# Down layers of four MLPs: 24 of 32 k tiles as seven block products in place of eight

## The chip, the cores and the metric

The program runs on one core of a Trainium2 chip. The metric is the device time of one execution in microseconds (us), as the median of repeated runs. The engines are TensorE (PE in the profile, its weight loads PEld), VectorE (DVE), ScalarE (ACT), GpSimd (POOL) and SyncE (SP), which issues the DMAs. [...]

## The reference

Two model blocks of two layers each work on 512 tokens of 1024 channels, with short convolution, sparse attention, latent attention and differential attention. Each of the four layers ends in an MLP with a squared ReLU, and this is the part that the change touches:

```python
# first block, both layers
x = x + jnp.square(jax.nn.relu(hm @ w_up[layer])) @ w_down[layer]
# second block, both layers
x = _layernorm(DEEPNORM_ALPHA * x + _sqrelu_mlp(x, ffn_w_up[i], ffn_w_down[i]), ...)
```

w_up is 1024 x 4096 and w_down 4096 x 1024, all in f32.

## The kernel before

Tokens lie in four tiles of 128. The residual stream x is kept in SBUF as [128 tokens, 4 tiles, 1024]. Every f32 product is made of three matmuls in the fp32r type: an operand is split into a high part, a ScalarE copy into fp32r (line 95, tiles named ...h), and a low part, a VectorE subtraction (line 96, tiles named ...l). Then high x high, high x low and low x high are accumulated in a PSUM bank. All matmuls are issued by line 91. The split tiles come from one pool of six pairs of 128x1024, which up weights, down weights and r2 parts share; a pair is free when the last matmul that reads it is done. One pair is held by the memory keys of the second layer while the first MLP runs.

An MLP has two stages. The up stage (dense_b, line 221) makes 16 units of 256 hidden channels: a unit's weights are two blocks of 512 KB, its 48 matmuls of 128x512 fill the banks pus and put one after the other, ScalarE takes the ReLU (line 679), and VectorE multiplies it with the bank into r2 (line 680), which is kept for all 4096 channels in four tiles of 128x4096. While a unit runs, the weights of the next are loaded and split. The down stage (dense_a, line 165) then runs over 32 k tiles of 128 hidden channels: a row block of w_down of 512 KB is loaded and split, two k tiles of r2 are split at a time, and for each of the four token tiles six matmuls of 128x512 go to two banks; eight banks hold the whole result until the last k tiles. After that each token tile is added to x or goes into the LayerNorm with the factor ALPHA on x (lines 323 and 330).

The order within an engine is set by a scheduler that follows the order of the program text and takes an instruction when its inputs and buffers are there by its own costs. In each engine's queue instructions run strictly in that order. SP issues all loads; the raw weights have three buffers.

Of the kernel before, what the change touches and what calls it, by code (L numbers as in the profile page):

```python
# [10 lines left out]
FT = mybir.dt.float32  # L11
# [3 lines left out]
OP = mybir.AluOpType  # L15
# [17 lines left out]
def model_kernel(ctx: ExitStack, tc: tile.TileContext, I, out, tap=lambda *a: None, stop=0):  # L33
# [79 lines left out]
    def r16(name, dtype=FR):  # L113
        return big.tile([P, 4096], dtype, name=name, tag="r16")
# [50 lines left out]
    def dense_a(nK, lhs, weights, chunks, evac, tail=4, ntok=MT, late=None, ahead=3, hook=None):  # L165

        nch = len(chunks)
        dst = {}

        def alloc(t):  # L170
            if t in dst:
                return
            if nch == 2:
                if t == 0:
                    rot["S"] = rot["T"] = 0
                dst[t] = list(bankST("acc")) if t < 3 else [bankB("acc"), bankB("acc")]
            else:
                dst[t] = [bankT("acc") if t % 2 else bankS("acc")]

        W = {}  # L180

        def step(k, t, cs=range(nch)):
            alloc(t)
            wh, wl = W[k]
            lh, ll = lhs(k, t)
            for a, b, st, sp in ((lh, wh, k == 0, False), (lh, wl, False, False), (ll, wh, False, k == nK - 1)):
                for c in cs:
                    c0, c1 = chunks[c]
                    mm(dst[t][c][:, :c1 - c0], a, b[:, c0:c1], st, sp)

        head = max(0, nK - tail)
        k0 = 0
        if late is not None:
            k0 = min(ahead, nK)
            for k in range(k0):
                W[k] = weights(k)
            for t in range(ntok):
                if t == 2:
                    late()
                for k in range(k0):  # L200
                    step(k, t)
        for k in range(k0, head):
            W[k] = weights(k)
            for t in range(ntok):
                step(k, t)
        k0 = max(k0, head)
        for k in range(k0, nK):
            W[k] = weights(k)
        if hook:
            hook()  # L210
        for t in range(ntok):
            if nch == 2 and t == ntok - 1:
# [112 lines left out]
    def layer_norm(t, ps, gb, bb, alpha=ALPHA, dst=None):  # L325
        xt = x[:, t, :]
        st = small(4, "ln")
        for c in range(2):
            xc = x[:, t, c * 512:(c + 1) * 512]
            nc.vector.scalar_tensor_tensor(xc, xc, alpha, ps[c], op0=OP.mult, op1=OP.add, accum_out=st[:, c:c + 1])  # L330
        nmu = st[:, 2:3]
        nc.vector.scalar_tensor_tensor(nmu, st[:, 0:1], st[:, 1:2], ndiv, op0=OP.add, op1=OP.mult)
        sq = w4("sq")
        nc.scalar.activation(sq, xt, AF.Square, bias=nmu, accum_out=st[:, 3:4])
        xg = w4("xg")
        nc.vector.scalar_tensor_tensor(xg, xt, nmu, gb, op0=OP.add, op1=OP.mult)
        r = rstd_of(st[:, 3:4], 1, D, 1e-5)
        for c in (slice(0, 512), slice(512, D)) if dst is not None else (slice(0, D),):
            nc.vector.scalar_tensor_tensor(xt[:, c], xg[:, c], r, bb[:, c], op0=OP.mult, op1=OP.add)
            if dst is not None:  # L340
                nc.sync.dma_start(dst[:, c], xt[:, c])
# [325 lines left out]
                todo.append(unit)  # L667
        return todo

    def mlp(L, box, w_up, w_down, after, hook=None, tail=3):  # L670
        xT = box["xT"]
        r2 = [r16("r2", FT).rearrange("p (k n) -> p k n", k=8) for _ in range(4)]
        ups = dense_b(xT[0], xT[1], 8, 16,
                      lambda u, k0: wblk(w_up, 4096, k0, 4, u * 256, 256, base=L * D * 4096), box["late"], True)
        for u in range(16):
            ps = next(ups)
            rr = w4("rr").rearrange("p (a n) -> p a n", a=2)
            for m in range(2):
                nc.scalar.activation(rr[:, m, :], ps[m], AF.Relu)  # L679
                nc.vector.scalar_tensor_tensor(r2[u // 4][:, (2 * u) % 8 + m, :], ps[m], 0.0, rr[:, m, :],  # L680
                                               op0=OP.max, op1=OP.mult)
        rs = {}

        def lhs(k, t):
            if k not in rs:
                h, l = pair("r")
                h, l = (v.rearrange("p (a n) -> p a n", a=2) for v in (h, l))
                split(h, l, r2[k // 8][:, k % 8:k % 8 + 2, :])
                rs[k], rs[k + 1] = (h[:, 0], l[:, 0]), (h[:, 1], l[:, 1])
            return rs[k][0][:, t * P:(t + 1) * P], rs[k][1][:, t * P:(t + 1) * P]  # L690

        dense_a(32, lhs, lambda k: wcols(w_down, D, k, 0, D, base=L * 4096 * D), C2, after, tail=tail, hook=hook)


    rope_tab = {}
# [689 lines left out]
    after, box = ln_next(ln_rows("mix", 0), 1.0)  # L1385
    w_out(I["mla_w_o_2"], 0, oT, after, range(4, 8))
    tap("x4", x)
    after, box2 = ln_next(ln_rows("ffn", 0))
    mlp(0, box, I["ffn_w_up_2"], I["ffn_w_down_2"], after)
    xT = box2["xT"]  # L1390
    tap("x5", x)
    if stop == 3:
# [167 lines left out]
    rows_ = ln_rows("ffn", 1)  # L1560

    def after(t, ps):
        layer_norm(t, ps, *rows_, dst=out[0, t * P:(t + 1) * P, :])

    mlp(1, box, I["ffn_w_up_2"], I["ffn_w_down_2"], after, tail=4)


def bucket_onehots():
# [45 lines left out]
```

## Time and profile before

| what | value |
|---|---|
| median of 3 runs | 2416.0 us (2415.68 to 2416.78) |
| the profiled execution | 2416.09 us |
| its span, first to last instruction | 2414.3 us |
| mean granted TensorE clock | 0.995 of full speed |
| TensorE busy | 2358.9 us, 98% |
| VectorE busy | 1221.3 us, 51% |
| ScalarE busy | 969.4 us, 40% |
| GpSimd busy | 270.7 us, 11% |

A matmul's record overlaps the next one, since matmuls are pipelined; the pitch from start to start tells what one costs. In the rows below, a name such as wl<-raw,wh says what is written and what is read, a bracket at the end of a row of the timeline says how long the engine had been idle and what ended that, and GB/s is the last column of a row by stretch.

### The profile page before, as it was taken

The page shows a single profiled execution, that of the slowest core. Times are in us where ns is not written, and L with a number is a line of the kernel's source. Part 1 is how long each engine was busy: PE and PEld are TensorE (multiplying, and loading weights), DVE is VectorE, ACT ScalarE, POOL GpSimd, SP SyncE. Part 2 cuts the span into 40 slices and gives each one's busy share as a digit, 9 for nine tenths or more (in the row PEclk, how much of TensorE's full clock was granted, in tenths as well). Part 3 has the DMA queues.
Part 4 walks back from the last instruction along what each step waited for, and adds up shares of the span by engine and source line. Part 5 has one row for each costly group of instructions (what it writes and reads, how often), then busy time and mean ns, then how long its engine had stood idle before and what let it go on. Part 6 is the DMA issues. An engine that isn't in the chain of part 4 may idle for free.

```text
span 2414.3 us, 32343 instructions
## 1 busy us (share of the span) xinstructions
PE 2358.9 (98%) x12735; PEld 2030.2 (84%) x12735; DVE 1221.3 (51%) x2250; ACT 969.4 (40%) x1749; POOL 270.7 (11%) x458
## 2 busy tenths in 40 slices
PE   8999999999988999999999999999999999999998
PEld 7888888888887888888888888888889997888887
DVE  6564333336678973333347773333366668433334
ACT  5342322225458853332225543222235555323222
POOL 1110000000345520000001100000011222000000
PEclk9999999999999999999999999999999999999999
DMA  6233332334201133323221233323321222432332
GB/s 205 82 109 90 105 104 80 96 96 131 75 27 36 45 102 105 91 85 96 96 84 47 63 114 105 103 80 96 97 90 53 61 63 79 123 104 79 96 96 70
DMA packets 149540, 214.91 MB, mean 89 GB/s; under 512 B 12571, under 2 KB 119390, under 8 KB 149387
## 3 DMA queue, kind: packets, MB, share of 16 engines
q1 hardware_dynamic: 148718, 212.54, 28.5%
q8 instruction: 100, 1.64, 0.3%
q14 instruction: 54, 0.43, 0.1%
q10 hardware_dynamic: 668, 0.30, 0.0%
HBM read 210.68 MB, written 2.13 MB: 88 GB/s over the span
## 4 chain that ended last, share of the span: by engine, by line
PE 88%; DVE 5%; ACT 3%; POOL 2%; DMA 1%; issue 1%; ACTq 0%; DVEq 0%; POOLq 0%
PE pus L91 16%; PE put L91 16%; PE acc L91 13%; PE accs L91 12%; PE acct L91 12%; PE df L91 5%; PE sp L91 2%; PE wo L91 2%; PE pT L473 2%; PE do L91 1%; POOL z L457 1%; POOL rstd L129 1%; PE no L91 1%; PE qks L91 1%; PE lo L91 1%
## 5 line engine op out<-in xcount | busy, mean ns | idle before, releaser
L96 DVE TENSOR_TENSOR wl<-raw,wh 128x1024 fp32r<-128x1024 f32 (+3 forms) x363 | 436.9, 1205 | 528.3 <-ACT wh L95 525.7
L95 ACT ACTIVATE wh<-raw 128x1024 fp32r<-128x1024 f32 (+3 forms) x363 | 375.3, 1038 | 566.4 <-PE acc L91 317.5
L129 POOL TENSOR_TENSOR rstd<-var,mhalf 128x1 f32<-128x1 f32 (+3 forms) x91 | 77.7, 854 | 1712.2 <-DVE var L127 1712.2
L91 PE MATMUL pus<-xTh,wh 128*128 128x512 f32 (+1 forms) x664 | 241.5, 366 | 1.9 <-ACT xTh L95 1.0
L91 PE MATMUL pus<-xTh,wl 128*128 128x512 f32 (+1 forms) x664 | 240.9, 364 | 0.0
L91 PE MATMUL put<-xTh,wl 128*128 128x512 f32 (+1 forms) x664 | 240.7, 363 | 0.0
L91 PE MATMUL pus<-xTl,wh 128*128 128x512 f32 (+1 forms) x664 | 240.4, 364 | 0.3 <-DVE xTl L96 0.3
L91 PE MATMUL put<-xTl,wh 128*128 128x512 f32 (+1 forms) x664 | 240.3, 364 | 0.0
L91 PE MATMUL put<-xTh,wh 128*128 128x512 f32 (+1 forms) x664 | 239.9, 364 | 0.0
L96 DVE TENSOR_TENSOR rl<-r,rh 128x1024 fp32r<-128x1024 f32 x64 | 78.2, 1224 | 160.7 <-ACT rh L95 160.7
L91 PE MATMUL accs<-wh,rh 128*128 128x512 f32 x384 | 149.8, 390 | 0.9 <-ACT rh L95 0.9
L91 PE MATMUL acct<-wh,rh 128*128 128x512 f32 x384 | 149.8, 390 | 0.0
L91 PE MATMUL accs<-wl,rh 128*128 128x512 f32 x384 | 149.5, 389 | 0.0
L91 PE MATMUL accs<-wh,rl 128*128 128x512 f32 x384 | 149.3, 389 | 0.0
L91 PE MATMUL acct<-wl,rh 128*128 128x512 f32 x384 | 149.3, 389 | 0.0
L91 PE MATMUL acct<-wh,rl 128*128 128x512 f32 x384 | 149.1, 389 | 0.0
L680 DVE SCALAR_TENSOR_TENSOR r<-pus,rr 128x512 f32<-128x512 f32 x64 | 44.3, 691 | 203.7 <-ACT rr L679 203.7
L91 PEld LDWEIGHTS pus<-xTh,wh 128*128 128x128 f32 x664 | 125.2, 189 | 22.9 <-ACT xTh L95 2.3
L91 PEld LDWEIGHTS put<-xTh,wl 128*128 128x128 f32 x664 | 125.3, 189 | 19.7
L91 PEld LDWEIGHTS pus<-xTl,wh 128*128 128x128 f32 x664 | 125.1, 189 | 20.0 <-DVE xTl L96 0.5
L91 PEld LDWEIGHTS pus<-xTh,wl 128*128 128x128 f32 x664 | 125.3, 189 | 19.4
L91 PEld LDWEIGHTS put<-xTh,wh 128*128 128x128 f32 x664 | 125.0, 189 | 19.5
(451 smaller groups left out, 5119.3 us busy)
## 6 DMA issues: line engine op xcount, KB each, us to landing
raw<-in_w_up_dram SPq DMA_DIRECT2D x64, 512.0 KB, 3.8
raw<-in_w_down_dram SPq DMA_DIRECT2D x64, 512.0 KB, 3.4
raw<-in_ffn_w_up_dram SPq DMA_DIRECT2D x64, 512.0 KB, 4.5
raw<-in_ffn_w_down_dram SPq DMA_DIRECT2D x64, 512.0 KB, 3.5
raw<-in_diff_w_qkv_dram SPq DMA_DIRECT2D x24, 512.0 KB, 3.6
raw<-in_a_w_in_dram SPq DMA_DIRECT2D x20, 512.0 KB, 3.6
raw<-in_w_out_dram SPq DMA_DIRECT2D x16, 512.0 KB, 4.0
raw<-in_mem_w_kv_dram SPq DMA_DIRECT2D x8, 512.0 KB, 4.6
```

Of the source, the lines that this page charges most:

```text
L91: return nc.tensor.matmul(o, a, b, start=start, stop=stop, skip_group_check=True)
L95: nc.scalar.activation(h, src, AF.Copy)
L96: nc.vector.tensor_sub(l, src, h.bitcast(FT))
L129: nc.gpsimd.tensor_tensor(r, v, mhalf[:np_, :w], op=OP.pow)
L457: nc.gpsimd.tensor_scalar(z[:, b, :nq], z[:, b, :nq], rc[:, b:b + 1], sc[b], op0=OP.mult, op1=OP.mult)
L473: nc.tensor.transpose(T[:, c0:c0 + P], z[:, b, kt * P:(kt + 1) * P], ident)
L680: nc.vector.scalar_tensor_tensor(r2[u // 4][:, (2 * u) % 8 + m, :], ps[m], 0.0, rr[:, m, :], op0=OP.max, op1=OP.mult)
```

## The change

The first 24 of the 32 k tiles of a down layer are taken in three groups of eight. A group is a product of 512 tokens x 1024 channels with 1024 x 1024 weights, cut in two each way: blocks a11 to a22 of r2 (256 tokens x 512 channels) and b11 to b22 of w_down (512 x 512). In place of the eight block products there are seven, made of sums of blocks, with some results accumulated in the same banks: the Winograd form of Strassen's scheme. A group becomes ready with every fourth up unit, and its seven products are woven between the following four units, two behind each and one behind the last. A product has its operands (a load or block sums, then the splits sa and sb of one block of each side), 24 matmuls into two banks (sA or sB by turns), and an evacuation that adds the two banks to a quarter of x, which takes the factor ALPHA where a quarter is first met. A group is kept until the next one: r2 has two tiles in place of four, and the weights' four blocks are in two tiles rw, overwritten by sums. The last 8 k tiles are done by dense_a as before. In the second block the LayerNorm behind the MLP has the factor 1.0.

```diff
+    def seven(buf, k0, src, base, first, alpha):
+        a11, a12, a21, a22 = (buf[:, 4 * k:4 * k + 4, 256 * t:256 * t + 256] for t, k in ((0, 0), (0, 1), (1, 0), (1, 1)))
+        slots = [r16("rw", FT).rearrange("p (s k n) -> p s k n", s=4, k=2) for _ in range(2)]
+        b11, b12, b22, b21 = ([slots[q // 2][:, q % 2 * 2 + i] for i in range(2)] for q in range(4))
...
+        def load(b, kh, nh):
+            for i in range(2):
+                nc.sync.dma_start(b[i], dram(src, base + (k0 + 4 * kh + 2 * i) * P * D + nh * 512,
+                                             [[D, P], [P * D, 2], [1, 512]]))
+        def minus(dst, a, b):
+            for i in range(2):
+                nc.vector.tensor_sub(dst[i], a[i], b[i])
...
+        def product(key, b, a, op, fresh, rows, cols):
+            def operands():
+                if op:
+                    op()
+                o["a"] = parts(st[a] if isinstance(a, str) else a, 4, "sa")
+                o["b"] = [parts(v, 2, "sb") for v in b]
+            def products():
+                if fresh:
+                    bank[key] = [(bankF if key == "A" else bankB)("s" + key) for _ in range(2)]
+                ps = bank[key]
+                ah, al = o["a"]
+                for k in range(4):
+                    bh, bl = (v[:, k % 2, :] for v in o["b"][k // 2])
+                    for n, (p, q) in enumerate(((ah, bh), (ah, bl), (al, bh))):
+                        for t in range(2):
+                            mm(ps[t], p[:, k, t * P:(t + 1) * P], q, fresh and k == 0 and n == 0, k == 3 and n == 2)
+            def evacuation():
+                for t in range(2):
+                    xc = x[:, 2 * rows + t, cols * 512:cols * 512 + 512]
+                    if first and alpha is not None and (rows, cols) not in seen:
+                        nc.vector.scalar_tensor_tensor(xc, xc, alpha, bank[key][t], op0=OP.mult, op1=OP.add)
+                    else:
+                        nc.vector.tensor_add(xc, xc, bank[key][t])
...
+        def op5():
+            minus(b11, b12, b11)
+            st["s"] = quarter()
+            nc.vector.tensor_add(st["s"], a21, a22)
+            load(b21, 1, 0)
+        def op6():
+            minus(b11, b22, b11)
+            nc.vector.tensor_sub(st["s"], st["s"], a11)
+        def op3():
+            nc.vector.tensor_sub(st["s"], a12, st["s"])
+        def op7():
+            minus(b12, b22, b12)
+            st["s3"] = quarter()
+            nc.vector.tensor_sub(st["s3"], a11, a21)
...
+        return loads, [product("A", b11, a11, lambda: load(b22, 1, 1), True, 0, 0),
+                       product("B", b11, "s", op5, True, 1, 1),
+                       product("A", b11, "s", op6, False, 0, 1),
+                       product("B", b22, "s", op3, False, 0, 1),
+                       product("A", b12, "s3", op7, False, 1, 1),
+                       product("B", b21, a12, None, True, 0, 0),
+                       product("A", b21, a22, lambda: minus(b21, b21, b11), False, 1, 0)]
-    def mlp(L, box, w_up, w_down, after, hook=None, tail=3):
+    def mlp(L, box, w_up, w_down, after, hook=None, tail=3, alpha=None):
...
-        r2 = [r16("r2", FT).rearrange("p (k n) -> p k n", k=8) for _ in range(4)]
+        rot["on"] = False
         for u in range(16):
+            if u % 4 == 0:
+                if u:
+                    loads, todo = seven(r2, 2 * u - 8, w_down, wd, u == 4, alpha)
+                    loads()
+                r2 = r16("r2", FT).rearrange("p (k n) -> p k n", k=8)
             ps = next(ups)
...
+            for _ in range(2 if u % 4 < 3 else 1):
+                if todo:
+                    operands, products, evacuation = todo.pop(0)
+                    operands()
+                    for e in last:
+                        e()
+                    products()
+                    last[:] = [evacuation]
...
-        dense_a(32, lhs, lambda k: wcols(w_down, D, k, 0, D, base=L * 4096 * D), C2, after, tail=tail, hook=hook)
+        dense_a(8, lhs, lambda k: wcols(w_down, D, 24 + k, 0, D, base=wd), C2, after, tail=tail, hook=hook)
```

What the scheduler makes of it is seen in the queues. First, TensorE in the first MLP, where unit 4 ends and unit 5 begins; before, the units follow each other:

```order
L91 MATMUL put<-xTh,wh 128x512
L91 MATMUL put<-xTl,wh 128x512
L91 MATMUL put<-xTh,wl 128x512
L91 MATMUL pus<-xTh,wh 128x512
L91 MATMUL pus<-xTl,wh 128x512
```

Now, from the middle of product 1 of the first group (sA) to the first use of a low weight half (sbl) in product 2 (sB):

```order
L91 MATMUL sA<-sbl,sah 128x512 x2
L91 MATMUL sA<-sbh,sal 128x512 x2
L91 MATMUL sA<-sbh,sah 128x512 x2
...
L91 MATMUL pus<-xTh,wh 128x512
L91 MATMUL pus<-xTl,wh 128x512
L91 MATMUL pus<-xTh,wl 128x512
L91 MATMUL pus<-xTh,wh 128x512
L91 MATMUL sB<-sbh,sah 128x512 x2
L91 MATMUL pus<-xTl,wh 128x512
...
L91 MATMUL sB<-sbl,sah 128x512 x2
```

Ten matmuls of product 1, four of unit 5, two of product 2 and four more of unit 5 stand there; the rest of product 2, unit 5 and product 3 follow.

Second, VectorE at the same place of the first MLP; before, the splits of the up weights (wl) and the writes of r2 (r):

```order
L680 SCALAR_TENSOR_TENSOR r_1991<-pus,rr 128x512
L96 TENSOR_TENSOR wl<-raw,wh 128x1024 x2
L680 SCALAR_TENSOR_TENSOR r_1991<-put,rr 128x512
L680 SCALAR_TENSOR_TENSOR r_1991<-pus,rr 128x512
L96 TENSOR_TENSOR wl<-raw,wh 128x1024 x2
```

Now, from the split of product 1's second weight pair to that of product 3's first (L688 are sums of weight blocks, L739 and L742 of r2 blocks, L723 evacuations):

```order
L96 TENSOR_TENSOR sbl<-rw,sbh 128x1024
L688 TENSOR_TENSOR rw<-rw 128x1024
L96 TENSOR_TENSOR sal<-sq,sah 128x1024
L688 TENSOR_TENSOR rw<-rw 128x1024
L96 TENSOR_TENSOR sbl<-rw,sbh 128x1024 x2
L723 TENSOR_TENSOR x<-x,sA 128x512 x2
L688 TENSOR_TENSOR rw<-rw 128x1024
L96 TENSOR_TENSOR wl<-raw,wh 128x1024
...
L739 TENSOR_TENSOR sq<-sq,r_1990 128x1024
...
L742 TENSOR_TENSOR sq<-r_1990,sq 128x1024
L96 TENSOR_TENSOR sbl<-rw,sbh 128x1024 x2
```

Left out are a sum of weight blocks and a split of up weights, and between L739 and L742 two evacuations of sB with an r2 write between them and a split of a block sum.

Third, VectorE in the third MLP, around units 4 and 5. Before:

```order
L680 SCALAR_TENSOR_TENSOR r_12861<-put,rr 128x512
L680 SCALAR_TENSOR_TENSOR r_12862<-pus,rr 128x512
L96 TENSOR_TENSOR wl<-raw,wh 128x1024 x2
L680 SCALAR_TENSOR_TENSOR r_12862<-put,rr 128x512
L680 SCALAR_TENSOR_TENSOR r_12862<-pus,rr 128x512
```

Now, from the write of unit 4's first half to the split that product 2 uses first:

```order
L780 SCALAR_TENSOR_TENSOR r_13498<-pus,rr 128x512
L96 TENSOR_TENSOR sbl<-rw,sbh 128x1024
L688 TENSOR_TENSOR rw<-rw 128x1024 x2
L780 SCALAR_TENSOR_TENSOR r_13498<-put,rr 128x512
L96 TENSOR_TENSOR sal<-sq,sah 128x1024
L688 TENSOR_TENSOR rw<-rw 128x1024
L96 TENSOR_TENSOR sbl<-rw,sbh 128x1024
```

Here the split of product 1's second weight pair stands first, and TensorE's queue has products 1 and 2 of a group back to back, 24 matmuls each, with a whole up unit of 48 behind every two products.

## Rows read from the trace of the kernel before

**Rows 1.** page, engines: busy us (share of the span), instructions
```profile
span 2414.3 us, 32343 instructions
...
PE 2358.9 (98%) x12735; PEld 2030.2 (84%) x12735; DVE 1221.3 (51%) x2250; ACT 969.4 (40%) x1749; POOL 270.7 (11%) x458
```

**Rows 2.** page, chain that ended last: shares by engine, by line
```profile
PE 88%; DVE 5%; ACT 3%; POOL 2%; DMA 1%; issue 1%; ACTq 0%; DVEq 0%; POOLq 0%
...
PE pus L91 16%; PE put L91 16%; PE acc L91 13%; PE accs L91 12%; PE acct L91 12%; PE df L91 5%; PE sp L91 2%; PE wo L91 2%; PE pT L473 2%; PE do L91 1%; POOL z L457 1%; POOL rstd L129 1%; PE no L91 1%; PE qks L91 1%; PE lo L91 1%
```

**Rows 3.** busy time in MLP stretches: PE, PEld, DVE, ACT, POOL; clock, DMA
```profile
290.00:360.00 70.00, 70.00 (x311) 57.95 (x310) 25.51 (x27) 20.79 (x27) 0.00 (x0) 1.00 0.32 98
...
440.00:550.00 110.00, 110.00 (x487) 91.09 (x486) 37.01 (x31) 30.75 (x31) 0.00 (x0) 1.00 0.30 96
...
2260.00:2360.00 100.00, 100.00 (x443) 82.84 (x442) 33.33 (x28) 27.65 (x27) 0.00 (x0) 1.00 0.30 95
```

**Rows 4.** timeline, first down layer: start, length, instruction, wait before it
```profile
402.72 0.68 DVE L680 SCALAR_TENSOR_TENSOR r<-put,rr 128x512 f32<-128x512 f32 x1
...
403.45 0.19 PEld L91 LDWEIGHTS acct<-wh,rh 128*128 128x128 f32 x1 [0.26 <-DVE r L680]
...
405.66 0.63 PE L91 MATMUL acc<-wh,rl 128*128 128x512 f32 x2
...
406.12 0.39 PE L91 MATMUL accs<-wh,rh 128*128 128x512 f32 x1
...
406.32 1.06 ACT L95 ACTIVATE wh<-raw 128x1024 fp32r<-128x1024 f32 x1 [4.29 <-PE acc L91]
...
407.42 1.23 DVE L96 TENSOR_TENSOR wl<-raw,wh 128x1024 fp32r<-128x1024 f32 x1 [4.01 <-ACT wh L95]
...
409.98 0.39 PE L91 MATMUL acct<-wh,rl 128*128 128x512 f32 x1
```

**Rows 5.** groups by line and shape: count, busy us, mean ns, idle before
```profile
L96 DVE TENSOR_TENSOR wl<-raw,wh 128x1024 fp32r<-128x1024 f32 x341 | 418.3, 1228 | 515.7 <-ACT wh L95 513.4 <-issue 0.6 <-PE wo L91 0.6
...
L95 ACT ACTIVATE wh<-raw 128x1024 fp32r<-128x1024 f32 x341 | 359.2, 1057 | 549.2 <-PE acc L91 305.1 <-PE put L91 205.6 <-issue 10.9
...
L680 DVE SCALAR_TENSOR_TENSOR r<-pus,rr 128x512 f32<-128x512 f32 x64 | 44.3, 691 | 203.7 <-ACT rr L679 203.7
...
L339 DVE SCALAR_TENSOR_TENSOR x<-xg,rstd,gb 128x1024 f32<-128x1024 f32 x12 | 15.4, 1284 | 5.9 <-POOL rstd L129 5.8
...
L323 DVE TENSOR_TENSOR x<-x,accs 128x512 f32<-128x512 f32 x12 | 8.2, 684 | 13.5 <-PE accs L91 13.5
...
L746 DVE TENSOR_TENSOR qr<-rope 128x256 f32<-128x256 f32 x8 | 3.3, 417 | 0.1
...
L679 ACT ACTIVATE rr<-pus 128x512 f32<-128x512 f32 x64 | 38.3, 598 | 249.1 <-PE pus L91 249.1
```

**Rows 6.** DMA issues: count, KB each, us to landing
```profile
raw<-in_w_down_dram SPq DMA_DIRECT2D x64, 512.0 KB, 3.4
...
raw<-in_w_out_dram SPq DMA_DIRECT2D x16, 512.0 KB, 4.0
```

**Rows 7.** busy time by stretch around a pause of TensorE; clock
```profile
134.00:136.00 2.00, 0.97 (x9) 0.72 (x7) 0.94 (x2) 1.56 (x7) 0.00 (x0) 1.00 0.00 0
136.00:138.00 2.00, 0.99 (x4) 0.74 (x4) 1.29 (x3) 2.00 (x5) 1.25 (x3) 0.92 0.01 4
138.00:140.00 2.00, 2.00 (x9) 1.81 (x9) 1.85 (x3) 1.57 (x3) 0.60 (x2) 0.50 0.05 8
140.00:142.00 2.00, 2.00 (x8) 1.62 (x8) 1.34 (x2) 1.80 (x4) 0.00 (x0) 0.72 0.47 147
```

**Rows 8.** timeline of TensorE in that stretch
```profile
136.91 0.87 PE L91 MATMUL mo<-mpth,mkvl 128*128 128x256 f32 x2 [1.94 <-ACT mpth L95]
...
138.43 0.63 PE L91 MATMUL put<-xTh,wh 128*128 128x512 f32 x1
...
138.85 0.63 PE L91 MATMUL put<-xTl,wh 128*128 128x512 f32 x1
```

More of the change, by code (lines that the diff above doesn't have):

```diff
@@ L668, in w_out_part, with parts, quarter, loads @@
         return todo
-    def mlp(L, box, w_up, w_down, after, hook=None, tail=3):
+    def seven(buf, k0, src, base, first, alpha):
+        a11, a12, a21, a22 = (buf[:, 4 * k:4 * k + 4, 256 * t:256 * t + 256] for t, k in ((0, 0), (0, 1), (1, 0), (1, 1)))
+        slots = [r16("rw", FT).rearrange("p (s k n) -> p s k n", s=4, k=2) for _ in range(2)]
+        b11, b12, b22, b21 = ([slots[q // 2][:, q % 2 * 2 + i] for i in range(2)] for q in range(4))
+        bank = {}
+        seen = set()
+        st = {}
+        def load(b, kh, nh):
[5 more added lines that the diff above has]
+                nc.vector.tensor_sub(dst[i], a[i], b[i])
+        def parts(v, k, name):
+            h, l = pair(name)
+            h, l = (c.rearrange("p (k n) -> p k n", k=k) for c in (h, l))
+            split(h, l, v)
+            return h, l
+        def product(key, b, a, op, fresh, rows, cols):
+            o = {}
+            def operands():
[20 more added lines that the diff above has]
+                        nc.vector.tensor_add(xc, xc, bank[key][t])
+                seen.add((rows, cols))
+            return operands, products, evacuation
+        def quarter(name="sq"):
+            return w4(name).rearrange("p (k n) -> p k n", k=4)
+        def op5():
[12 more added lines that the diff above has]
+            nc.vector.tensor_sub(st["s3"], a11, a21)
+        def loads():
+            load(b11, 0, 0)
+            load(b12, 0, 1)
+        return loads, [product("A", b11, a11, lambda: load(b22, 1, 1), True, 0, 0),
[5 more added lines that the diff above has]
+                       product("A", b21, a22, lambda: minus(b21, b21, b11), False, 1, 0)]
@@ L671, in mlp @@
+    def mlp(L, box, w_up, w_down, after, hook=None, tail=3, alpha=None):
         xT = box["xT"]
-        r2 = [r16("r2", FT).rearrange("p (k n) -> p k n", k=8) for _ in range(4)]
+        wd = L * 4096 * D
         ups = dense_b(xT[0], xT[1], 8, 16,
                       lambda u, k0: wblk(w_up, 4096, k0, 4, u * 256, 256, base=L * D * 4096), box["late"], True)
+        rot["on"] = False
+        todo = []
+        last = []
+        r2 = None
         for u in range(16):
+            if u % 4 == 0:
[3 more added lines that the diff above has]
+                r2 = r16("r2", FT).rearrange("p (k n) -> p k n", k=8)
@@ L679, in mlp @@
                 nc.scalar.activation(rr[:, m, :], ps[m], AF.Relu)
-                nc.vector.scalar_tensor_tensor(r2[u // 4][:, (2 * u) % 8 + m, :], ps[m], 0.0, rr[:, m, :],
+                nc.vector.scalar_tensor_tensor(r2[:, (2 * u) % 8 + m, :], ps[m], 0.0, rr[:, m, :],
                                                op0=OP.max, op1=OP.mult)
+            for _ in range(2 if u % 4 < 3 else 1):
[6 more added lines that the diff above has]
+                    last[:] = [evacuation]
+        for e in last:
+            e()
+        rot["on"] = True
         rs = {}
@@ L687, in lhs @@
                 h, l = (v.rearrange("p (a n) -> p a n", a=2) for v in (h, l))
-                split(h, l, r2[k // 8][:, k % 8:k % 8 + 2, :])
+                split(h, l, r2[:, k:k + 2, :])
                 rs[k], rs[k + 1] = (h[:, 0], l[:, 0]), (h[:, 1], l[:, 1])
             return rs[k][0][:, t * P:(t + 1) * P], rs[k][1][:, t * P:(t + 1) * P]
-        dense_a(32, lhs, lambda k: wcols(w_down, D, k, 0, D, base=L * 4096 * D), C2, after, tail=tail, hook=hook)
+        dense_a(8, lhs, lambda k: wcols(w_down, D, 24 + k, 0, D, base=wd), C2, after, tail=tail, hook=hook)
     rope_tab = {}
@@ L1387, in model_kernel @@
     tap("x4", x)
-    after, box2 = ln_next(ln_rows("ffn", 0))
-    mlp(0, box, I["ffn_w_up_2"], I["ffn_w_down_2"], after)
+    after, box2 = ln_next(ln_rows("ffn", 0), 1.0)
+    mlp(0, box, I["ffn_w_up_2"], I["ffn_w_down_2"], after, alpha=ALPHA)
     xT = box2["xT"]
@@ L1562, in after @@
     def after(t, ps):
-        layer_norm(t, ps, *rows_, dst=out[0, t * P:(t + 1) * P, :])
-    mlp(1, box, I["ffn_w_up_2"], I["ffn_w_down_2"], after, tail=4)
+        layer_norm(t, ps, *rows_, alpha=1.0, dst=out[0, t * P:(t + 1) * P, :])
+    mlp(1, box, I["ffn_w_up_2"], I["ffn_w_down_2"], after, tail=4, alpha=ALPHA)
 def bucket_onehots():
```

## The prediction

> **What bounds the kernel now.** I read the engine totals first. TensorE is busy for 2358.9 of 2414.3 us, VectorE for half of the span, ScalarE for 40% [rows 1]. Since a busy TensorE need not be one that sets the time, I then read the chain that ended last: 88% of it is TensorE, and the named parts of it are the up products (pus, put) and the down products (acc, accs, acct), together 69% of the span [rows 2]. Third, the busy time by stretch, for a piece of an up layer and two of down layers: in all of them TensorE is busy 100% of the stretch at full clock, VectorE only 33 to 36%, GpSimd not at all, and the DMA engines run at 0.30 to 0.32 [rows 3]. So in these stages nothing but the number of matmuls counts, and the other engines have room. The pitch of the matmuls comes from the timeline: from 406.12 to 409.98 us stand 17 steps of 128x512, so 3.86 / 17 = 0.227 us each; a matmul's own 0.39 us overlaps the next one [rows 4].
>
> **What goes.** One group of eight k tiles took 8 x 4 x 2 x 3 = 192 matmuls. Seven products of 4 x 3 x 2 = 24 make 168. That is 24 fewer in each of three groups of each of four MLPs, 288 in all, of the same shape, on a path where TensorE never waits: 288 x 0.227 = 65.4 us.
>
> The Trainium skill, "TensorE: Matmul & The Clock Gate", section "Wait — 56ns, not 53.3ns?", gives 215.7 ns from start to start for 512 columns at full clock. By it the 288 would be worth 62.1 us; the trace has 0.227 us, 5% more, and I go by the trace.
>
> **What is added.** Per group, 21 splits (7 of block sums of r2, 14 of weight halves) stand where 12 stood (8 weights, 4 of r2): 9 more, each a ScalarE copy of 1.057 us and a VectorE subtraction of 1.228 [rows 5]. New are 12 sums of 128x1024 on VectorE and 14 reads of a PSUM bank into x (0.684 us, as line 323 does it [rows 5]). A sum with a plain f32 result of that size is not in the trace. From below it is bounded by the split, 1.228; from above by four times the small one of line 746, 4 x 0.417 = 1.67; the nearest at the full size and with an f32 result is line 339 with 1.284 [rows 5]. I take 1.23.
>
> The budget of one group, woven with four up units, is then: TensorE (192 + 168) x 0.227 = 81.8 us. VectorE (21 + 8) x 1.228 = 35.6, sums 14.7, evacuations 9.6, the up units' eight r2 writes 5.5: together 65.4 us, 80%. ScalarE 29 x 1.057 + 8 x 0.6 = 35.5 us. VectorE has room on the average and little at any one place; as it works in order, what counts is how long its queue is ahead of each split that a product waits for.
>
> **Where TensorE waits, first MLP.** The memory keys of the next layer hold one of the six split buffer pairs here, so the scheduler put pieces of the next up unit between the products. Between the first use of the low half of product 1's second weight pair and that of product 2 stand 10 + 4 + 2 + 4 = 20 matmuls, 4.54 us; on VectorE between the same two splits a sum, a split, a sum and the split that is wanted, 4 x 1.228 = 4.91. TensorE waits 0.37 us. From there to product 3's first split stand 61 matmuls (22 of product 2, 13 pus, 24 put, 2), 13.85 us, against nine operations of 1.228, four evacuations and an r2 write, 14.48 us: 0.63 us. Product 1 itself waits for a copy, an activation, an r2 write and a split behind the up unit's end, about 0.2. Products 4 and 6 wait for the evacuations in front of their split: a bank's last matmul ends 0.06 us before the next stream starts, then 0.03 + 2 x 0.684 + 1.228 + 0.05 makes 2.6 us against 11 matmuls, 2.5: 0.1 each. The hand-overs in these sums are those of the timeline: 0.03 us from a matmul's end to ScalarE, 0.04 on to VectorE, 0.05 back to TensorE [rows 4]. Together 1.4 us, three times: 4.2.
>
> **The other three MLPs.** With all six pairs products 1 and 2 stand back to back. The split of product 1's second pair ends 0.4 us before product 1 starts (its copy needs the weight pair that the put half returns at its eleventh of 24 matmuls: 13 x 0.227 before the end). Behind it stand two sums, an r2 write, a split, a sum and product 2's split, 5 x 1.228 + 0.69 = 6.83, so it is ready 6.4 + 0.05 us after the start of product 1; TensorE is there after 26 matmuls, 5.9 us. Wait 0.56 us, nine times: 5.0. Between the later products stand 48 up matmuls, 10.9 us, and I count no wait.
>
> **Loads.** They stay 512 KB each and are as many as before; in rows of 2 KB, as w_out's, which land in 4.0 us against 3.4 for w_down [rows 6]. The next group's loads wait on SP for the last sum of the old one, with up loads queued behind them; both are wanted a unit (10.9 us) later, and are costed at nothing. GpSimd has no queue here. LayerNorm only changes a factor.
>
> **Sum.** -65.4 + 4.2 + 5.0 = -56.2 us on the profiled execution's 2416.1 us (span 2414.3 and 1.8 around it), which is the median, 2416.0. Forecast 2360 us. If nothing waited: 2350.7.
>
> **Rivals.** (a) VectorE is later than counted. With sums of 1.67 the six sums on the counted ways of the first MLP add 2.7 us per group and the three of the others 1.3: 8 + 12 = 20 us. With a hand-over as long as the wait of 0.26 us at the start of a down layer [rows 4] at each of 84 products, 21 us. Either gives 2380, both 2401. For it speaks that 80% leaves little; against it that such rows keep their length in every stretch.
>
> (b) The slower side: VectorE's queue is one operation late at every product. It works in order, and an evacuation that has to wait for TensorE's last matmul holds the split behind it, which the next product wants. Then 84 x 1.228 = 103 us come on top: 2463. It decides from a mean wait of (65.4 - 9.2) / 84 = 0.67 us more per product. Against it: most evacuations stand behind the splits of the next product.
>
> (c) The loads of a group (four of 512 KB) land one behind the other, 4 x 4.0 = 16 us instead of within the 10.9 us of an up unit: 5.1 us in 12 groups, 61 us, 2421: no change. Against it: DMA engines at 0.3 busy [rows 3].
>
> (d) The new waits cost the clock. After a pause of 1.94 us at 135 us the granted clock went to 0.50, that is 1.2 GHz, and 0.72 in the 2 us behind [rows 7], and matmuls of 128x512 stood 0.42 us apart [rows 8]; some 1.7 us are lost at such a place. Once per group this is 21 us, 2381; at each of 84 products 143 us, 2503. Against it: in that stretch TensorE worked for 49% of 4 us, whereas here the longest wait counted is 0.63 us between long runs. The same page of the Trainium skill, "Part 1: The HAM clock gate", says that the clock is halved when the array has been idle and comes back with sustained work; the trace agrees, with 0.50 after the pause and 1.00 before.
>
> **How the numbers follow.** Chances: forecast 0.75 (own range 2350 to 2376), (a) 0.14, (b) 0.05, (c) 0.03, (d) 0.03. The range goes from 2349 (no wait, and the 0.26 us at the start of the down layers gone too) to 2388, which takes in half of (a). A change of 0.2% is what a measurement of this kernel can tell: 4.8 us. Faster takes in the forecast, (a) and part of (d): 0.90; the same 0.04, from (c) and the edge of (a); slower 0.06, from (b) and the rest of (d).
>
> **What would show it.** Right: 288 fewer matmuls, pitch 0.227 us in the woven stage, no idle time of TensorE over 1 us there, its waits naming the sbl splits and 5 to 20 us in all; VectorE 1221 + 108 x 1.228 + 144 x 1.23 + 168 x 0.684 = some 1645 us, ScalarE 969 + 114 = 1083. Wrong: sums far from 1.23 us, waits for rw loads, clock below 1.00 in the woven stretches, or idle time at most products.

## The result, and the profile after

The changed kernel takes 2353.0 us (median of 4 runs, 2352.0 to 2356.7) beside 2416.4 us for the kernel before on the same chip (4 runs): ratio 0.974, 95% interval 0.972 to 0.976. That is 63.4 us, where 56.2 were forecast; 2360 was predicted with a range of 2349 to 2388. In a later comparison the same kernel, unedited, came to 2353.5 us.

Of the page of the changed kernel, its span, the engine totals and the chain that ended last, by engine:

```profile
span 2350.3 us, 32274 instructions
PE 2293.5 (98%) x12447; PEld 1971.0 (84%) x12447; DVE 1608.7 (68%) x2670; ACT 1078.4 (46%) x1857; POOL 269.9 (11%) x458
PE 88%; DVE 4%; ACT 3%; POOL 2%; DMA 1%; issue 1%; ACTq 0%; SPq 0%; POOLq 0%; DVEq 0%
```

Against [rows 1] TensorE is busy for 65.4 us less and its matmuls are 288 fewer; the span is 64.0 us shorter. TensorE's 88% of the chain is what it was [rows 2]: the same engine sets the time, with less to do. The gain lies where the edit is: from its first up matmul to its last down matmul the first MLP takes 341.4 us before (236.54 to 577.98) and 326.7 after (235.15 to 561.84), 14.8 less, and the other three take 15.8, 15.7 and 15.7 less. That is 61.9 us; the rest of the 63.4 lies outside the MLPs. A matmul comes with a weight load, so 288 of each are gone, and the runs do not tell the two apart. The woven stages of the four MLPs, by busy time (PE, PEld, DVE, ACT, POOL; then clock, DMA share, GB/s):

```profile
280.00:515.20 235.20, 235.20 (x1032) 191.82 (x1031) 178.79 (x183) 99.20 (x108) 0.00 (x0) 1.00 0.26 83
927.70:1162.10 234.40, 234.40 (x1034) 193.44 (x1033) 178.70 (x190) 98.77 (x108) 0.00 (x0) 1.00 0.26 84
1453.00:1688.00 235.00, 235.00 (x1036) 193.99 (x1035) 176.93 (x183) 99.21 (x108) 0.00 (x0) 1.00 0.26 85
2063.00:2297.50 234.50, 234.50 (x1034) 193.54 (x1033) 176.57 (x182) 98.97 (x107) 0.00 (x0) 1.00 0.26 85
```

In [rows 3] VectorE was at 33 to 36% in such stretches; here it is at 76%, and TensorE is as full as before, at full clock. PE busy hides small waits: these rows are at 100%, though there are some. They show on the weight loads. From the list of waits, what the loads for bank B waited for (us in all, times, the longest):

```profile
PEld sB L91 <- DVE sbl L96: 3.8, 17, 0.3
PEld sB L91 <- ACT sbh L95: 1.9, 9, 0.2
```

And from the view of the tile sA, the only thing that those for bank A waited for (us, times):

```profile
  DVE sbl L96: 0.9, 3
```

These are 29 waits of 0.15 us and more at 84 products, none over 0.33 us, 6.6 us together; 20 of them lie in the first MLP. What TensorE loses by them is less: from the first product's first matmul to the first of the last eight k tiles the stages take 235.55, 234.43, 234.37 and 234.43 us. The same 1032 matmuls take 233.92 us where nothing waits (the last three MLPs of the kernel without sums, below). So the waits cost 1.6 us in the first MLP and 0.5 in each of the others, 3.1 in all.

Nine of the waits, all in the first MLP at products 2, 4 and 6, are for ScalarE's copy of the high half (sbh), which the prediction did not count. At product 4 of the first group that copy starts when a matmul of product 3 returns the buffer pair, and the weight load waits for it:

```profile
306.98 2.01 ACT L95 ACTIVATE sbh<-rw 128x1024 fp32r<-128x1024 f32 x2 [1.21 <-PE sA L91]
...
308.09 0.30 PEld L91 LDWEIGHTS sB<-sbh,sah 128*128 128x128 f32 x2 [0.21 <-ACT sbh L95]
```

The new operations, by line and shape (count, busy us, mean ns, idle before them):

```profile
L96 DVE TENSOR_TENSOR sbl<-rw,sbh 128x1024 fp32r<-128x1024 f32 x168 | 203.1, 1220 | 93.2 <-ACT sbh L95 90.9 <-DMA rw<-in_ffn_w_down_dram 2.3
L688 DVE TENSOR_TENSOR rw<-rw 128x1024 f32<-128x1024 f32 x96 | 116.0, 1218 | 0.8
L723 DVE TENSOR_TENSOR x<-x,sA 128x512 f32<-128x512 f32 x84 | 54.3, 681 | 3.7 <-PE sA L91 2.8
```

The loads that have a new shape (count, KB each, us to landing):

```profile
rw<-in_w_down_dram SPq DMA_DIRECT2D x48, 512.0 KB, 6.7
rw<-in_ffn_w_down_dram SPq DMA_DIRECT2D x48, 512.0 KB, 8.0
```

Sums (1.218 us) and evacuations (0.681; these read a PSUM bank, one of TensorE's accumulation banks, and add it to x) are what the prediction took. The loads are not: medians of 6.7 and 8.0 us to landing, where w_out's landed in 4.0 [rows 6]. Only one wait for them shows in the 168 splits, 2.3 us on VectorE.

### The profile page after: what moved, and what is told of

Its sections match the earlier page's. It is cut to its first block, busy times and chain, and to the rows that moved or that the text cites. A ratio compares the mean times of both kernels' runs of the same rounds, so it can differ in the third digit from the quotient of the medians.

```text
span 2350.3 us, 32274 instructions
## 1 busy us (share of the span) xinstructions
PE 2293.5 (98%) x12447; PEld 1971.0 (84%) x12447; DVE 1608.7 (68%) x2670; ACT 1078.4 (46%) x1857; POOL 269.9 (11%) x458
## 4 chain that ended last, share of the span: by engine, by line
PE 88%; DVE 4%; ACT 3%; POOL 2%; DMA 1%; issue 1%; ACTq 0%; SPq 0%; POOLq 0%; DVEq 0%
PE pus L91 17%; PE put L91 17%; PE sA L91 11%; PE sB L91 8%; PE acc L91 8%; PE df L91 5%; PE accs L91 4%; PE acct L91 4%; PE sp L91 2%; PE wo L91 2%; PE pT L473 2%; POOL z L457 1%; PE do L91 1%; POOL rstd L129 1%; PE no L91 1%
## 5 line engine op out<-in xcount | busy, mean ns | idle before, releaser
L96 DVE TENSOR_TENSOR wl<-raw,wh 128x1024 fp32r<-128x1024 f32 (+3 forms) x267 | 318.1, 1196 | 176.6 <-ACT wh L95 173.8
L95 ACT ACTIVATE wh<-raw 128x1024 fp32r<-128x1024 f32 (+3 forms) x267 | 273.6, 1031 | 265.6 <-PE acc L91 86.9
L96 DVE TENSOR_TENSOR sbl<-rw,sbh 128x1024 fp32r<-128x1024 f32 x168 | 203.1, 1220 | 93.2 <-ACT sbh L95 90.9
L95 ACT ACTIVATE sbh<-rw 128x1024 fp32r<-128x1024 f32 x168 | 176.8, 1058 | 176.1 <-PE put L91 84.1
L779 ACT ACTIVATE rr<-pus 128x512 f32<-128x512 f32 x64 | 38.3, 598 | 224.9 <-PE pus L91 224.9
L91 PEld LDWEIGHTS put<-xTl,wh 128*128 128x128 f32 x664 | 124.9, 189 | 19.7
L438 ACT ACTIVATE z<-z,mx 128x128 f32<-128x128 f32 (+1 forms) x192 | 106.5, 556 | 26.7 <-DVE mx L435 25.2
L91 PE MATMUL sA<-sbl,sah 128*128 128x512 f32 x384 | 118.6, 390 | 0.0
L91 PE MATMUL sA<-sbh,sal 128*128 128x512 f32 x384 | 118.3, 389 | 0.0
L91 PE MATMUL sA<-sbh,sah 128*128 128x512 f32 x384 | 118.2, 389 | 0.0
```

Source lines behind the costliest of these rows:

```text
L91: return nc.tensor.matmul(o, a, b, start=start, stop=stop, skip_group_check=True)
L438: nc.scalar.activation(z[:, b, :nq], z[:, b, :nq], AF.Exp, scale=-1.0, bias=mx[:, b:b + 1], accum_out=sm[:, b:b + 1])
```

## The experiments

Theory: the time is set by the number of matmuls, and VectorE's work hides behind them. Rivals: the weave itself gives the gain; VectorE's queue costs at every product; the sums are on the path.

**The matmuls put back.** Same weave, eight ordinary products in place of seven, the eighth behind the fourth unit; their list is the core of the edit. In this kernel x also enters the second block's MLPs without its factor alpha; that instruction takes 0.68 us with and without it.

```diff
-        return loads, [product("A", b11, a11, lambda: load(b22, 1, 1), True, 0, 0),
-                       product("B", b11, "s", op5, True, 1, 1),
...
+        return loads, [product("A", b11, a11, None, 0, 0, 0),
+                       product("A", b21, a12, lambda: load(b12, 0, 1), 1, 0, 0),
...
```

> The weave stays (same places between the up units, evacuations straight into x), but each group is eight ordinary block products of 24 matmuls, with no sums: 192 matmuls per group as in the kernel before, 24 splits and 8 evacuations on VectorE. Theory (the gain is the 288 matmuls left out): 288 x 0.227 = 65.4 us come back on 2352, less at most the 2.6 us of waits that the changed kernel has: 2415 to 2418, level with the kernel before. Rival (the weaving itself gives the gain, since TensorE no longer waits for a down stage's weights and the evacuations go early): 2352 to 2370.

Measured: 2419.1 us, ratio to before 1.0014 (1.0004 to 1.0023). The page:

```profile
PE 2362.8 (98%) x12735; PEld 2028.9 (84%) x12735; DVE 1451.7 (60%) x2490; ACT 1116.5 (46%) x1893; POOL 270.1 (11%) x458
```

With as many matmuls as before ([rows 1]) the time is level with the kernel before, 2416.2 us beside it: 2.9 us more, and 1 us past the expectation. From first up to last down matmul the last three MLPs take what they took, to 0.05 to 0.13 us; the first takes 2.6 us more, by waits between its products. So the weave gives nothing by itself. The 288 matmuls are worth 66.1 us between the medians of these two kernels, and 64.8 us by the four MLPs alone.

**The sums left out.** All else stays; the products are made of unsummed blocks.

```diff
-                       product("B", b11, "s", op5, True, 1, 1),
-                       product("A", b11, "s", op6, False, 0, 1),
+                       product("B", b11, a21, lambda: load(b21, 1, 0), True, 1, 1),
+                       product("A", b11, a22, None, False, 0, 1),
```

> The twelve sums of each group are left out (the blocks of r2 and of the weights enter the seven products as they are), all else stays: 144 operations of VectorE fewer. Theory (VectorE is hidden behind TensorE): 144 x 1.135 = 163 us of VectorE's work gone and only the 2.6 us of waits to win: 2350 to 2355, level with the changed kernel. Rival (the sums stand on the path, as each is wanted by the next product): half of one operation at each of the 60 products with a sum already gives 34 us, 2319.

Measured: 2352.4 us, ratio to before 0.973 (0.971 to 0.975), level with the changed kernel. VectorE does 144 operations and 157.6 us less:

```profile
PE 2296.6 (98%) x12447; PEld 1976.5 (84%) x12447; DVE 1451.1 (62%) x2526; ACT 1080.1 (46%) x1857; POOL 270.4 (11%) x458
```

The third MLP's woven stage, its first matmul and the first one behind it, by the timeline, first of this kernel and then of the changed one:

```profile
1456.58 0.62 PE L91 MATMUL sA<-sbh,sah 128*128 128x512 f32 x2
...
1690.50 0.39 PE L91 MATMUL accs<-wh,rh 128*128 128x512 f32 x1
```

```profile
1453.64 0.61 PE L91 MATMUL sA<-sbh,sah 128*128 128x512 f32 x2
...
1688.02 0.39 PE L91 MATMUL accs<-wh,rh 128*128 128x512 f32 x1
```

233.92 against 234.38 us; the second and the fourth take 233.92 too. In the first MLP the stage still takes 234.89 against 235.55: the waits at products 2, 4 and 6 stay, without any sum. So the sums cost 2.1 us of the 3.1 and no more. (The expectations of the other runs speak of 2.6 us of waits, worked out with a pitch of 0.2268 us; this stage gives 0.22667 per matmul, and so 3.1.)

**More work for VectorE, in three doses.** The subtraction behind a split is done twice: at one, two or all three splits of each product.

```diff
                 o["a"] = parts(va, 4, "sa")
+                nc.vector.tensor_sub(o["a"][1], va, o["a"][0].bitcast(FT))
```

> At each of the 84 products the subtraction that gives the low half of the block of r2 is done twice, so VectorE has one operation of 1.22 us more right in front of the splits of the weights. Theory (VectorE works in order but has some 20 us of room in each group of 81.8; only the few close places wait): 67 of 81.8 us per group, and 1.135 us more at three close places in each group of the first MLP and at one in each group of the others, (9 + 9) x 1.135 = 20 us at most, less what the scheduler puts in between: 2353 to 2372. Rival (b) of the prediction (one operation late is paid at every product): 84 x 1.135 = 95 us, 2447.

> At each of the 84 products the subtractions of both weight halves are done once more behind the second: two operations of VectorE more per product, 14 per group. Theory (the queue has 81.8 - 59 = 22.8 us of room per group and TensorE waits only when that is used up): 59 + 15.9 = 74.9 us, so still hidden but for the close places, 2354 to 2366. Rival (the loss grows evenly with each operation added; three more per product cost 31 us): two thirds of that, 2374.

> Each of the 252 splits of the products has its subtraction twice: three operations of VectorE more at each product, 21 in a group. Theory: VectorE needs 59 + 21 x 1.135 = 83 us per group where TensorE needs 81.8, so here VectorE becomes the bound: at least 12 x 1.2 = 14 us, and with the start of each MLP, where its queue is not yet full, up to 50: 2366 to 2402, with TensorE idle at most products. Rival (paid at every product): 252 x 1.135 = 286 us, 2638. Rival (VectorE has nothing to do with it): 2352.

Measured: 2355.9 us (0.976, 0.974 to 0.977), 2360.5 (0.977, 0.975 to 0.978), 2383.5 (0.987, 0.986 to 0.989). The second MLP's woven stage in the three, by busy time as above, one row of each, and for the third dose also the stage behind it:

```profile
936.20:1170.80 234.60, 234.60 (x1034) 193.27 (x1033) 201.80 (x217) 100.87 (x111) 0.00 (x0) 1.00 0.27 86
```

```profile
935.30:1170.60 235.30, 235.30 (x1033) 192.93 (x1032) 222.40 (x225) 99.12 (x108) 0.00 (x0) 1.00 0.27 84
```

```profile
941.60:1175.90 234.30, 230.68 (x1011) 188.87 (x1009) 232.28 (x233) 95.21 (x106) 0.00 (x0) 1.00 0.25 81
1175.90:1229.00 53.10, 53.09 (x230) 43.80 (x231) 31.93 (x50) 16.18 (x20) 0.00 (x0) 0.94 0.24 77
```

VectorE is at 86%, 94.5% and 99% of the stage. 84 and 168 added operations cost some 3 and 7 us by the medians, the first hardly more than single runs differ by. By the stages themselves it is less: in the last three MLPs they take 234.6 us with the first dose and 235.3 to 235.5 with the second, 0.1 to 0.2 and 0.9 to 1.1 more than in the changed kernel; the rest of the 3 and 7 us lies in the first MLP and in stages without products. At 99% the stage has 1010 matmuls in its time instead of 1032; the other 22 fall to the stage behind it, which grows from 45.1 to 53 us. Three steps of the same size cost 3, 5 and 23 us: neither of the rivals' prices (95 us for the first dose, an even 10 per dose) is there. VectorE is hidden until it is nearly full.

**The weave taken out of the code.** All seven products of a group are called behind one up unit.

```diff
-            for _ in range(2 if u % 4 < 3 else 1):
+            for _ in range(7):
```

> All seven products of a group are called behind the first up unit that follows it, and then three up units stand alone; instructions, loads and sums are the same in number. Theory (the weave is what hides VectorE): through the seven products VectorE needs 33 x 1.135 + 14 x 0.60 = 45.9 us where TensorE has 168 x 0.227 = 38.1 and some 18 to 26 up matmuls that the scheduler puts between, 4.1 to 5.9: 2 to 8 us of waits in each of 12 groups, 24 to 96 us, 2376 to 2448, and if TensorE's clock falls in the waits, more. Rival (only the sum over a group counts, 59 of 81.8 us): 2352 to 2358.

Measured: 2358.1 us (2354.0 to 2360.1), ratio 0.977 (0.975 to 0.979). The theory's price was wrong. One group of the third MLP, the stretch with the seven products and the one behind it, by busy time:

```profile
1453.90:1497.50 43.60, 43.60 (x192) 35.60 (x191) 40.93 (x42) 21.07 (x22) 0.00 (x0) 1.00 0.13 48
1497.50:1535.70 38.20, 38.20 (x170) 31.62 (x169) 20.34 (x22) 13.14 (x16) 0.00 (x0) 1.00 0.52 167
```

Of the timeline, operations of VectorE ahead of that stretch:

```profile
1445.87 1.21 DVE L688 TENSOR_TENSOR rw<-rw 128x1024 f32<-128x1024 f32 x1
1447.00 1.22 DVE L734 TENSOR_TENSOR sq<-r 128x1024 f32<-128x1024 f32 x1
...
1449.88 1.22 DVE L747 TENSOR_TENSOR sq<-r 128x1024 f32<-128x1024 f32 x1
...
1452.28 1.22 DVE L96 TENSOR_TENSOR sbl<-rw,sbh 128x1024 fp32r<-128x1024 f32 x1 [1.18 <-ACT sbh L95]
1453.42 2.35 DVE L688 TENSOR_TENSOR rw<-rw 128x1024 f32<-128x1024 f32 x2
```

The expectation set all 45.9 us of VectorE's work against the stretch of the products. But three of the sums shown and a split are done before the first product starts at 1453.9, the first of two more sums has been started, and the last evacuations come behind it; 40.9 us are left in 43.6, 94%, with an r2 write and two splits of up weights among them, and TensorE has no pause that the row would show. The woven stages take 235.3 to 235.9 us, 3 us more than the changed kernel's in all four. So the exact places of the products matter little too.

**A buffer pair held.** In the last three MLPs one of the six split buffer pairs is kept, as the memory keys keep one in the first.

```diff
+        held = None
+        if hold:
+            held = pair("hold")
...
+                nc.gpsimd.tensor_tensor(z[:, q:q + 1], held[q].bitcast(FT)[:, 0:1], r2[:, 7, 511:512], op=OP.add)
```

> In the last three MLPs one of the six split buffer pairs is held from the first up unit to the last, as the memory keys hold one in the first MLP; two small memsets and two 128x1 operations on GpSimd per MLP are all that is added. Theory (with five pairs the scheduler puts up matmuls between products 1 and 2, and their close places wait): the woven stage of all four MLPs comes to 235.5 us, as in the first MLP now, with 1.5 us of waits each, 6.0 in all where the changed kernel has 2.6: 2353 to 2358. Rival (the first MLP's stage is longer for another reason): the other three stay at 234.4.

Measured: 2356.1 us, ratio 0.975 (0.973 to 0.976). The third MLP's stage, as above:

```profile
1456.68 0.62 PE L91 MATMUL sA<-sbh,sah 128*128 128x512 f32 x2
...
1692.18 0.39 PE L91 MATMUL accs<-wh,rh 128*128 128x512 f32 x1
```

235.50 instead of 234.38; the four are 235.7, 235.6, 235.5 and 235.6. The first MLP's extra 1.1 us is the missing pair and the order that follows from it. The difference in the medians, 3 us, agrees, though it is no larger than single runs of one kernel differ.

**The sums on GpSimd.**

```diff
             for i in range(2):
-                nc.vector.tensor_sub(dst[i], a[i], b[i])
+                nc.gpsimd.tensor_sub(dst[i], a[i], b[i])
```

> The twelve sums of each group go from VectorE to GpSimd, which is idle in these stages. How long GpSimd takes for 128x1024 no row shows. Theory: VectorE was hidden, so nothing is won; GpSimd is hidden too while three sums in a row (those in front of product 2) take less than the 5.9 us from product 1's start to where product 2 wants them, that is up to 2 us each: 2350 to 2355. At 4 us each, 3 x 4 - 5.9 = 6 us are lost in each of 12 groups, 72 us. Rival (VectorE's queue costs more than the waits show): up to 10 us faster than the changed kernel, 2342 to 2348.

Measured: 2394.8 us, ratio 0.991 (0.989 to 0.992): 42 us slower than the changed kernel. What its products waited for:

```profile
PEld sB L91 <- DVE sbl L96: 35.5, 33, 2.3
```

The groups by line on GpSimd and VectorE:

```profile
L688 POOL TENSOR_TENSOR rw<-rw 128x1024 f32<-128x1024 f32 x96 | 279.5, 2919 | 601.6 <-DVE sbl L96 589.5 <-issue 10.9
L739 POOL TENSOR_TENSOR sq<-sq,r 128x1024 f32<-128x1024 f32 x12 | 40.5, 3376 | 0.0
...
L96 DVE TENSOR_TENSOR sbl<-rw,sbh 128x1024 fp32r<-128x1024 f32 x168 | 282.1, 1689 | 86.4 <-ACT sbh L95 85.9
L96 DVE TENSOR_TENSOR sal<-sq,sah 128x1024 fp32r<-128x1024 f32 x48 | 92.8, 1932 | 15.9 <-ACT sah L95 15.2
```

And one place of the timeline on both engines:

```profile
956.01 6.72 POOL L688 TENSOR_TENSOR rw<-rw 128x1024 f32<-128x1024 f32 x2
...
957.05 6.76 DVE L96 TENSOR_TENSOR wl<-raw,wh 128x1024 fp32r<-128x1024 f32 x2
```

A sum that GpSimd made while VectorE stood idle:

```profile
272.86 2.39 POOL L734 TENSOR_TENSOR sq<-r 128x1024 f32<-128x1024 f32 x1 [45.28 <-DVE r L780]
```

A sum takes 2.9 us there as a mean, up to 3.4 by line. By the expectation's rule three in a row are then 3 x 2.9 - 5.9 = 2.8 us late, 34 us in 12 groups; 42 were lost, and the 2350 to 2355 expected were missed. By the matmuls' starts product 2 loses 2.4 to 2.7 us per group, near the rule; product 6 in the last three MLPs loses 0.4 and product 3 in the first 2.6, which the rule did not name. Nor did it count that the splits on VectorE grow too, from 1.22 to 1.69 and 1.93 us, and where two of each stand side by side, both engines take 3.4 us for one, against 2.39 and 1.22 alone. VectorE got no freer for the sums it gave away: 182.7 us of 240 in the second MLP's stage, 76% as before.

**All 32 k tiles as seven products.** VectorE has room and the seven products may stand in one place, so the last eight k tiles were tried as well, with each group woven 3, 2, 2 (the expectation speaks of the third alone), and the changed kernel again beside it. In the second block the LayerNorm also takes its row sum by a ScalarE pass of its own, since the evacuations no longer give it; the expectation does not name that.

```diff
-        dense_a(8, lhs, lambda k: wcols(w_down, D, 24 + k, 0, D, base=wd), C2, after, tail=tail, hook=hook)
+        for i, (operands, products, evacuation) in enumerate(group):
+            operands()
+            for e in last:
+                e()
+            if i == 6:
+                after(0, None)
+                after(1, None)
+            products()
+            last[:] = [evacuation]
```

> The last eight k tiles of each MLP are made of seven block products too, behind the last up unit, so 96 matmuls more go, 24 in each of the four MLPs. For that the third group is woven as 3, 2 and 2 products over three up units, which frees the weight buffers one unit earlier, and the norms behind an MLP read x after the last block has been added to it. By the number of matmuls alone: 96 x 0.227 = 21.8 us, 2331. Theory (without up units beside it VectorE bounds the last group): VectorE needs 33 x 1.135 + 14 x 0.60 = 45.9 us for it, some 6 of them ahead of the last up unit's end, against 38.1 us of TensorE, and the norms of the last two row tiles (two 128x1024 operations of 1.22 to 1.28 us and a share of the transposes' split each, some 6 us) stand behind it in the open, where today's last stage is 45.5 us in all: 46 to 54 us per MLP, so 2352 to 2386, not faster than the changed kernel. Rival (VectorE gets far enough ahead, as it did when the seven products were called in one place): 2331 to 2345.

> The changed kernel once more, unedited, beside the kernel above: 2350 to 2357 in its single runs, and the same 2.6 us of waits in the four woven stages (1.5 in the first MLP, 0.3 to 0.4 in the others). What differs between its two profiles is what one execution differs from another by, and no difference of that size between the kernels here is told as an effect.

Measured: 2387.7 us, ratio 0.988 (0.987 to 0.990), against 2353.5 and 0.974 (0.972 to 0.976) for the changed kernel again, whose woven stages came to 235.5, 234.4, 234.5 and 234.4. So 96 matmuls fewer, and 34 us slower. By stretch, the second MLP's last group, what follows the third MLP, and the end of the kernel:

```profile
1180.20:1224.80 44.60, 41.21 (x178) 32.90 (x177) 42.29 (x51) 23.43 (x26) 0.00 (x0) 0.96 0.00 1
1748.90:1790.00 41.10, 29.49 (x214) 28.14 (x212) 24.26 (x38) 17.84 (x32) 6.41 (x8) 0.79 0.29 92
2369.70:2386.20 16.50, 0.42 (x2) 0.00 (x0) 11.33 (x19) 6.37 (x12) 2.03 (x4) 0.59 0.34 127
```

From the timeline, the transposes behind the first MLP:

```profile
570.11 1.11 PE L287 MATMUL xts<-ident,xn 128*128 128x128 f32 x4 [5.42 <-DVE xn L301]
```

The changed kernel's stretches that answer to the last two:

```profile
1734.10:1775.20 41.10, 38.95 (x307) 38.09 (x306) 19.01 (x34) 12.60 (x23) 5.35 (x6) 0.96 0.25 81
...
2342.10:2350.30 8.20, 0.42 (x2) 0.00 (x0) 3.77 (x8) 1.24 (x2) 0.54 (x1) 0.65 0.34 128
```

The weave as 3, 2, 2 costs nothing: from the first product to the last up matmul the stages take 235.3, 234.2, 234.3 and 234.3 us. The last group takes 44.2 to 45.4 us from the last up matmul to the last product where the ordinary one takes 44.3 to 46.6: VectorE is busy for 42.3 of 44.6 and TensorE waits, as the theory had it. Then the norms stand in the open: TensorE pauses for 5.4 us at 564.7, it is idle for 11.6 of the 41.1 us behind the third MLP where the changed kernel has 2.2, and the kernel's end is 8.3 us longer. In the second block the added ScalarE pass, 1.05 us for each row tile, is part of that. The granted clock behind these pauses is lower, 0.79 in the 41 us behind the third MLP where the changed kernel has 0.96. Neither the clock nor the pass was in the expectation, and the result is just past its upper end; how much of the 34 us each costs was not separated.

## Why the prediction was right

**What goes: right.** 288 matmuls, 65.4 us of TensorE's busy time, and the matmuls put back bring 66.1, or 64.8 by the MLPs alone. Where nothing waits a matmul takes 233.92 / 1032 = 0.2267 us, the pitch that the prediction read from the trace.

**What is added: right in size.** Sums at 1.218 us against the 1.23 taken (bounds 1.23 to 1.67), evacuations 0.681 against 0.684, and the sums at 2.1 us in all, as the kernel without sums shows. VectorE's total came to 1608.7 us instead of 1645, for the reason that follows.

**Where TensorE waits: right in kind, mis-sized.** This is the term that failed: 9.2 us forecast, 3.1 measured. The prediction counted VectorE's queue by the length of its records, 1.228 us for each operation. Queued operations start closer than that. The changed kernel's VectorE around product 2 in the third MLP, and the weight load that waits for it:

```profile
1455.45 0.68 DVE L780 SCALAR_TENSOR_TENSOR r<-put,rr 128x512 f32<-128x512 f32 x1
1456.05 1.22 DVE L96 TENSOR_TENSOR sal<-sq,sah 128x1024 fp32r<-128x1024 f32 x1
1457.19 1.22 DVE L688 TENSOR_TENSOR rw<-rw 128x1024 f32<-128x1024 f32 x1
1458.32 1.22 DVE L96 TENSOR_TENSOR sbl<-rw,sbh 128x1024 fp32r<-128x1024 f32 x1
1459.46 0.68 DVE L721 SCALAR_TENSOR_TENSOR x<-x,sA 128x512 f32<-128x512 f32 x1
...
1459.59 0.30 PEld L91 LDWEIGHTS sB<-sbl,sah 128*128 128x128 f32 x2 [0.32 <-DVE sbl L96]
```

From start to start stand 1.14, 1.13 and 1.14 us behind records of 1.22, and 0.60 behind one of 0.68: a record overlaps the next by 0.08 to 0.09 us. The Trainium skill, "Perfetto Trace Analysis", section "DVE / Act Engine Instruction (TENSOR_ADD, Activation, etc)", has this: the recorded end is the acknowledged write, while the next instruction may begin to fetch once the one before has finished executing. The trace agrees, with 1.135 against 1.22. With 1.135 and 0.60 the prediction's own chains come out so: product 1 to 2 in the first MLP 4 x 1.135 = 4.54 us against 4.54 of matmuls (0.37 us late was forecast); product 2 to 3 there 13.2 against 13.85 (0.63 forecast); product 2 in the other MLPs 5 x 1.135 + 0.60 - 0.4 + 0.05 = 5.9 against 5.9 (0.56 forecast). By the matmuls' starts product 2 loses 0.08 to 0.11 us in the first MLP, product 3 at most 0.02, and product 2 in the others 0.13 to 0.19. So all but one of the places named were the right ones, and product 3, where the most was forecast, shows nothing. The short chains were sized well: product 1 of the first MLP loses 0.17 to 0.24 us against 0.2, products 4 and 6 lose 0.07 to 0.15 against 0.1, though not only by the evacuations named there: the copy sbh waits for its pair as well. The row that would have told this was in the trace before the change. The operation of VectorE just ahead of the first one of [rows 4]:

```profile
401.58 1.23 DVE L96 TENSOR_TENSOR rl<-r,rh 128x1024 fp32r<-128x1024 f32 x1 [1.50 <-ACT rh L95]
```

It is 1.23 us long, and the next starts 1.14 us behind it, at 402.72.

**Loads: right at nothing, wrong in length.** They land in 6.7 to 8.0 us instead of 4.0, and cost TensorE no wait that shows. Rows of 2 KB are not the reason, and only four of w_out's sixteen loads have them. In the kernel with eight products such loads, issued with no other load in the 6 us before, land in 3.8 and 3.9 us, those behind others in 6.7 to 9.0; in the changed kernel it is 5.4 to 6.1 behind two others and 7.3 to 8.1 behind four or five. The tile rw of the kernel with eight products, from 1016 to 1019 us:

```profile
DMA to landing us min/median/max: 3.8/3.8/3.8
```

So loads issued together land later, which is what rival (c) is about, but four of them take 8 us and not 16, and a unit's 10.9 us hides that.

**LayerNorm's factor and SP's queue: nothing seen.** From the first to the last matmul of the last eight k tiles the stages take 44.3 to 46.6 us, 0.8 to 3.1 more than their 192 matmuls; the 768 of before took 0.9 to 3.4 more.

**The rivals.** VectorE later than counted, and one operation late at each product: 84 real operations more cost 3 us, not 103, and the room that VectorE has between the products takes them up until the third dose fills it. The clock stayed at 1.00 in all woven stretches. The 7 us between forecast and result are 6 us of waits that did not come and 1 us within what one execution differs from the next. How large that is, the attention stage that the change doesn't touch shows. One stretch of it before the change, and the same one after:

```profile
699.30:713.40 14.10, 12.25 (x72) 11.55 (x72) 10.39 (x33) 10.13 (x30) 6.89 (x14) 0.76 0.01 2
```

```profile
683.00:694.80 11.80, 9.60 (x71) 8.49 (x71) 10.65 (x33) 10.04 (x30) 6.81 (x14) 1.00 0.01 2
```

The same work takes 2.3 us less at a granted clock of 1.00 than at 0.76; 2 us the other way stand between the third MLP's last down matmul and the next up matmul, 269.8 us before and 271.9 after.

## What to carry to other kernels

Where TensorE is full and another engine has room, fewer matmuls pay in full even at the price of many more operations on the other engine: here VectorE went from 33 to 36% of such a stretch to 76% for 3 us of waits, and could have gone to 94% for 4 to 7 more. That work paid beside other TensorE work; in the last group, where nothing stood beside it, 24 fewer matmuls gained 2 us at most and opened the norms behind it. Count a queue by the distance from start to start in the trace, not by the length of its records.

## What was not expected of the hardware

GpSimd and VectorE slow each other on 128x1024 operations with two inputs from SBUF, the working memory: where they ran side by side, 1.22 us on VectorE and 2.39 on GpSimd became 3.4 on both. The Trainium skill, "SBUF — State Buffer", section "SBUF: two separate sides", says that the two share a port pair that one instruction holds to its end while the other is blocked; the trace agrees: two operations of each take 7.8 us side by side (956.01 to 963.81), where one behind the other they would take 2 x (2.39 + 1.22) = 7.2. And a load of 512 KB that landed in 3.8 us with no other load ahead of it took 7.3 to 8.1 us behind four or five; the trace has the landing of only some of the loads.
